# Row normalisation of a 1024 x 4096 array: loads spread over the SyncE and the ScalarE queue

## The chip, the cores and the metric

One core of one Trainium2 chip. The metric is the device time of one execution in microseconds (us), as a median over several executions. The profile is of one execution and covers some 1.7 us less than that time.

## The reference

Each row of `x` (1024 x 4096, float32) is divided by its Euclidean norm:

```python
norm = np.sqrt(np.sum(x ** 2, axis=axis, keepdims=True) + eps)   # axis = -1
return (x / norm).astype(np.float32)
```

16.78 MB are read and 16.78 MB written; there is no reuse.

## The kernel before

The 1024 rows make 4 tiles of 128 partitions x 2 rows (4 MB each, 32 KiB to a partition). All four tiles have a buffer of their own, so nothing waits for a buffer.

```python
    for i in range(n_tiles):                       # 4 loads, all issued at once
        xt = io.tile([P, R, D], mybir.dt.float32)
        nc.sync.dma_start(out=xt.rearrange("p r d -> p (r d)"), in_=x[i])
        xts.append(xt)

    for i in range(n_tiles):
        xt = xts[i]
        ssq = stats.tile([P, R], mybir.dt.float32)
        for r in range(R):                         # ScalarE: squares and their sum
            nc.scalar.activation(out=sq, in_=xt[:, r], func=...Square,
                                 accum_out=ssq[:, r : r + 1])
        ...                                        # ScalarE: square root; VectorE: reciprocal
        for r in range(R):                         # VectorE: scale in place
            nc.vector.tensor_scalar_mul(
                out=xt[:, r], in0=xt[:, r], scalar1=rstd[:, r : r + 1]
            )
        nc.sync.dma_start(out=out_t[i], in_=xt.rearrange("p r d -> p (r d)"))
```

## Time and profile before

| | before |
|---|---|
| time, median | 84.22 us (84.21 to 84.26, 3 runs) |
| span of the profile | 82.5 us |
| DMA engines busy | 96% of the span |
| ScalarE / VectorE busy | 41% / 23% |
| moved | 33.55 MB, 1024 packets of 32 KiB and 128 tiny ones |

In a row of tenths, each digit is the busy share of a fortieth of the span (2.06 us here); 9 is 90% or more. A line of the timeline begins with the start and the length of a piece of work; in brackets stands how long its engine was idle before it, and what ended that. DVE is VectorE, ACT is ScalarE; SPq and ACTq are the instruction queues of SyncE and ScalarE, where a `DMA_DIRECT2D` line is the handing over (the issue) of a transfer. `xt<-in_x_dram` is a load, `out_dram<-xt` a store. A transfer is moved in packets, here of 32 KiB, by the 16 DMA engines, and it has landed when its last packet is reported done. The slack of a store is how much later it could be issued without a DMA engine having to wait for it. The lines themselves are in the prediction.

### The profile page before, as it was taken

The numbers are of one execution on the slowest core, as the hardware profiler recorded it, in microseconds if no ns is written. First come the engines' busy times: TensorE is split into PE (matmuls) and PEld (weight loads), VectorE is DVE, ScalarE is ACT, GpSimd is POOL, SyncE is SP. The second block draws the span as 40 slices with busy tenths as digits, with TensorE's granted clock in tenths as the row PEclk, the third lists the DMA queues.
The fourth block names the chain that finished last, engine by engine and source line by source line (L and its number), as shares of the span: only waits on it lengthen the run. The fifth ranks groups of instructions, "written<-read, shape, count | busy, mean of one in ns | idle before, by whom it ended". The sixth has DMA issues, their size and how long they took to land.

```text
span 82.5 us, 98 instructions
## 1 busy us (share of the span) xinstructions
DVE 19.2 (23%) x13; ACT 33.4 (41%) x22; POOL 0.2 (0%) x4
## 2 busy tenths in 40 slices
DVE  0000000000299019910498003990000000000000
ACT  6000006999799982999519996000000000000000
POOL 0000000000000000000000000000000000000000
DMA  6689998996999899899979989998998998899890
GB/s 175 286 365 445 508 397 365 508 461 302 508 493 397 381 508 413 350 508 461 302 302 461 493 381 397 508 413 350 508 445 381 445 508 381 381 508 413 365 493 0
DMA packets 1152, 33.55 MB, mean 407 GB/s; under 512 B 128, under 2 KB 128, under 8 KB 128
## 3 DMA queue, kind: packets, MB, share of 16 engines
q1 hardware_dynamic: 1152, 33.55, 96.0%
HBM read 16.78 MB, written 16.78 MB: 407 GB/s over the span
## 4 chain that ended last, share of the span: by engine, by line
DMA 50%; ACT 9%; DVE 3%; DVEq 3%; SPq 1%; issue 0%
DMA xt<-in_x_dram 50%; ACT sq L53 9%; DVE xt L70 3%; DVEq L104 3%; SPq L46 1%; ACT rstd L61 0%; DVE rstd L67 0%
## 5 line engine op out<-in xcount | busy, mean ns | idle before, releaser
L53 ACT ACTIVATE sq<-xt 128x4096 f32<-128x4096 f32 x8 | 28.9, 3617 | 16.5 <-DMA xt<-in_x_dram 16.4
L70 DVE TENSOR_SCALAR xt<-xt,rstd 128x4096 f32<-128x4096 f32 x8 | 18.5, 2350 | 0.1
L67 DVE RECIPROCAL rstd<-rstd 128x2 f32<-128x2 f32 x4 | 0.7, 166 | 35.5 <-ACT rstd L61 35.5
L53 ACT ACT_TABLE_LOAD x1 | 1.3, 1283 | 0.7 <-PEq L90 0.7
L53 ACT ACTIVATION_READ_ACCUMULATOR sq<-xt 128x1 f32 x8 | 1.5, 186 | 0.0
L61 ACT ACT_TABLE_LOAD x1 | 1.3, 1283 | 0.0
L61 ACT ACTIVATE rstd<-ssq,eps_t 128x2 f32<-128x2 f32 x4 | 1.2, 296 | 0.1
L41 DVE MEMSET eps_t<- 128x1 f32 x1 | 0.1, 59 | 0.8 <-PEq L90 0.8
L90 POOL MEMSET const-bfloat16-1.0<- 128x1 bf16 x1 | 0.1, 102 | 0.0
L90 POOL MEMSET const-uint8-127<- 128x1 uint8 x1 | 0.1, 102 | 0.0
L90 POOL MEMSET const-float32-0.0<- 128x1 f32 x1 | 0.1, 99 | 0.2 <-issue 0.2
L90 POOL MEMSET const-float32-1.0<- 128x1 f32 x1 | 0.1, 99 | 0.0
## 6 DMA issues: line engine op xcount, KB each, us to landing
xt<-in_x_dram SPq DMA_DIRECT2D x4, 4096.0 KB, 26.2
out_dram<-xt SPq DMA_DIRECT2D x4, 4096.0 KB, 26.4
```

The costliest lines, as they stand in the source:

```text
L41: nc.vector.memset(eps_t, eps)
L46: nc.sync.dma_start(out=xt.rearrange("p r d -> p (r d)"), in_=x[i])
L53: nc.scalar.activation(out=sq, in_=xt[:, r], func=mybir.ActivationFunctionType.Square, accum_out=ssq[:, r : r + 1],)
L61: nc.scalar.activation(out=rstd, in_=ssq, func=mybir.ActivationFunctionType.Sqrt, bias=eps_t,)
L67: nc.vector.reciprocal(out=rstd, in_=rstd)
L70: nc.vector.tensor_scalar_mul(out=xt[:, r], in0=xt[:, r], scalar1=rstd[:, r : r + 1])
L90: nc = _bacc.Bacc("TRN2", target_bir_lowering=False, num_devices=1)
L104: with _tile.TileContext(nc) as tc:
```

## The change

Two queues hand loads to the DMA engines instead of one: tiles 0 and 2 by SyncE, tiles 1 and 3 by ScalarE. The intent is to have two loads in progress at once. Stores stay on SyncE.

```diff
+    queues = (nc.sync, nc.scalar)
     xts = []
     for i in range(n_tiles):
-        xt = io.tile([P, R, D], mybir.dt.float32)
-        nc.sync.dma_start(out=xt.rearrange("p r d -> p (r d)"), in_=x[i])
+        xt = io.tile([P, R, D], F32)
+        queues[i % 2].dma_start(
+            out=xt.rearrange("p r d -> p (r d)"), in_=x_t[i]
+        )
         xts.append(xt)
```

Cut: renames, and the pool of statistics that goes from 4 buffers to `n_tiles`, which is also 4.

More of the change, by code (lines that the diff above doesn't have):

```diff
@@ L20 @@
     P = nc.NUM_PARTITIONS
+    F32 = mybir.dt.float32
     assert isinstance(axis, int) and axis in (-1, len(x.shape) - 1)
@@ L31 @@
     n_tiles = N // (P * R)
-    x = x.rearrange("(t p r) d -> t p (r d)", p=P, r=R)
+    x_t = x.rearrange("(t p r) d -> t p (r d)", p=P, r=R)
     out_t = out_flat.rearrange("(t p r) d -> t p (r d)", p=P, r=R)
@@ L36 @@
     scratch = ctx.enter_context(tc.tile_pool(name="scratch", bufs=1))
-    stats = ctx.enter_context(tc.tile_pool(name="stats", bufs=4))
-    sq = scratch.tile([P, D], mybir.dt.float32)
-    eps_t = scratch.tile([P, 1], mybir.dt.float32)
+    stats = ctx.enter_context(tc.tile_pool(name="stats", bufs=n_tiles))
+    sq = scratch.tile([P, D], F32)
+    eps_t = scratch.tile([P, 1], F32)
     nc.vector.memset(eps_t, eps)
+    queues = (nc.sync, nc.scalar)
     xts = []
     for i in range(n_tiles):
-        xt = io.tile([P, R, D], mybir.dt.float32)
-        nc.sync.dma_start(out=xt.rearrange("p r d -> p (r d)"), in_=x[i])
+        xt = io.tile([P, R, D], F32)
+        queues[i % 2].dma_start(
+            out=xt.rearrange("p r d -> p (r d)"), in_=x_t[i]
+        )
         xts.append(xt)
@@ L50 @@
         xt = xts[i]
-        ssq = stats.tile([P, R], mybir.dt.float32)
+        ssq = stats.tile([P, R], F32)
         for r in range(R):
@@ L58 @@
             )
-        rstd = stats.tile([P, R], mybir.dt.float32)
+        rstd = stats.tile([P, R], F32)
         nc.scalar.activation(
```

## The prediction

> **What bounds the kernel now.** I read first what limits the whole span, then whether any stage has another limit, then how much spare time the compute has. The page of the kernel before comes first: busy shares, the DMA row of the 40 slices, packets and queues.
>
> ```profile
> span 82.5 us, 98 instructions
> DVE 19.2 (23%) x13; ACT 33.4 (41%) x22; POOL 0.2 (0%) x4
> ...
> DMA  6689998996999899899979989998998998899890
> ...
> DMA packets 1152, 33.55 MB, mean 407 GB/s; under 512 B 128, under 2 KB 128, under 8 KB 128
> q1 hardware_dynamic: 1152, 33.55, 96.0%
> ```
>
> No compute engine reaches half the span, and the 16 DMA engines are busy for 96% of it, with no gap in the row of tenths except at the two ends. 128 of the packets are tiny (the completion marks); the other 1024 carry 33.55 MB, so 32 KiB each, 64 on each engine. A mean packet takes 0.96 x 82.5 x 16 / 1024 = 1.237 us; the single packet records of the steady stretches stand at 1.213 us. 64 x 1.213 = 77.6 us of the 82.5 us span is therefore time in which each DMA engine moves bytes at its steady rate, and 16 x 32 KiB / 1.213 us is 432 GB/s. The rest of the span (4.9 us) is: 1.7 us until the first packet starts, some 0.8 us because first packets take about 2 us, 0.7 us where loads give way to stores (the loads land 9.7 us apart, the last one 10.4 us after its forerunner), some 0.35 us from the last packet to its landing, and 0.8 us of closing down. Another 84.2 - 82.5 = 1.7 us of the measured time lies outside the profiled span.
>
> Next the DMA issues and the waits, for where transfers sit in the queue.
>
> ```profile
> xt<-in_x_dram SPq DMA_DIRECT2D x4, 4096.0 KB, 26.2
> out_dram<-xt SPq DMA_DIRECT2D x4, 4096.0 KB, 26.4
> ```
>
> All eight transfers go through the one SyncE queue. A transfer of 4 MB needs about 9.7 us alone, yet a store needs 26.4 us from issue to landing, because it stands behind two others. The stores are issued early and queue: the compute is far ahead of the DMA. The timeline gives the slack.
>
> ```profile
> 0.73 1.28 ACT L53 ACT_TABLE_LOAD   x1 [0.73 <-PEq L90]
> 0.73 1.91 SPq L46 DMA_DIRECT2D xt<-in_x_dram  x4
> ...
> 13.07 3.62 ACT L53 ACTIVATE sq<-xt 128x4096 f32<-128x4096 f32 x1 [11.05 <-DMA xt<-in_x_dram]
> ...
> 20.54 1.28 ACT L61 ACT_TABLE_LOAD   x1
> ...
> 22.78 3.62 ACT L53 ACTIVATE sq<-xt 128x4096 f32<-128x4096 f32 x1 [0.65 <-DMA xt<-in_x_dram]
> ...
> 30.79 4.62 DVE L70 TENSOR_SCALAR xt<-xt,rstd 128x4096 f32<-128x4096 f32 x2
> ...
> 42.99 3.62 ACT L53 ACTIVATE sq<-xt 128x4096 f32<-128x4096 f32 x1 [2.71 <-DMA xt<-in_x_dram]
> ...
> 51.00 4.62 DVE L70 TENSOR_SCALAR xt<-xt,rstd 128x4096 f32<-128x4096 f32 x2
> ```
>
> The squares start at 13.07, 22.78, 32.51 and 42.99, each time when a load has landed. The stores issue at 27.00, 35.44, 45.16 and 55.65, and land at 52.7, 62.3, 72.0 and 81.7. The store queue's data starts only when the loads are done, near 42.5, and store k's turn comes near 42.5, 52.2, 61.9 and 71.6. A store needs about 1.0 us from issue to first packet (first load: issue 0.73, packet 1.74). So the slack of the four is about 14.5, 15.7, 15.7 and 14.9 us. The chain of waits puts only half of the span on the loads and stops at the last store's issue; the row of DMA tenths is what shows that the stretch from 56 to 82 us is DMA alone.
>
> **What the Trainium skill says.** The page "DMA: Bandwidth & Descriptors", section "Issuing engines are not separate DMA queues", says that transfers started by ScalarE, SyncE or GpSimd all end on the same 16 DMA engines and interleave, and that several issuers save only the sequencer's issue time. The trace of before cannot test that, as it has one queue, but shows what there is to save: an issue takes 0.38 to 0.53 us while a transfer lasts 9.7 us. The section "Where 436 GB/s comes from" of the same page sets the ceiling on the SBUF side at 435.2 GB/s; this trace's 432 GB/s in the steady stretches is 99.3% of it, so it agrees and leaves nothing to gain in rate. Its section "Queues, rings and completion order" (arbitration) says that each DMA engine takes packets from the queues that have work in turn; no run here shows that yet, and the prediction of landing times rests on it. Last, the table of "Latency and other measured facts" reports slow copies where partition rows lie 4 MiB apart in HBM (103 GB/s against 207); this is a rival below.
>
> **The change part by part.**
> Renames, the type alias and the moved comment cost nothing. The stats pool goes from 4 buffers to one per tile; 1024 rows / (128 x 2) is 4 tiles, so it stays 4. Instruction counts stay: 8 transfers of 4 MB, 8 squares, 4 square roots, 4 reciprocals, 8 scalings.
>
> Issue: SyncE loses two load issues (about 0.9 us) and ScalarE gains two. They are ahead of ScalarE's first square, with the 1.28 us table load: some 2.2 us of its first 22 us. Nothing waits for either. The first load still leaves SyncE at 0.73, so the first packet still starts near 1.7. Cost on the path: 0.
>
> Landing order: tiles 0 and 1 now share each DMA engine packet by packet, then tiles 2 and 3. Two tiles are 16 packets per engine, 19.4 us. So tile 0, which landed at 13.0, lands at about 21.5 to 22.8, together with tile 1 (22.8 before); tiles 2 and 3 land together at about 42 to 43 (32.5 and 43.0 before). ScalarE's first wait grows from 11 to about 20 us.
>
> Compute: from the first square to the store's issue is 27.00 - 13.07 = 13.93 us for the first tile (it has the table load of the square root), and 35.44 - 22.78 = 12.66 us for a later one. ScalarE is held by the first tile for 9.06 us (13.07 to 22.13), by a later one for 7.78 us (22.78 to 30.56). VectorE's part (0.17 + 4.62) is shorter and never holds it up.
> - tile 0: 22.6 + 13.93, store issued at 36.5
> - tile 1: ScalarE free at 31.7, + 12.66 = 44.3
> - tile 2: landed near 42.7, + 12.66 = 55.4
> - tile 3: ScalarE free at 50.5, + 12.66 = 63.2
>
> The stores come 9.5, 8.9, 10.2 and 7.5 us later than before. Now against the DMA: the loads still need 32 packets per engine and end near 42.5; the stores' turns stay at 42.5, 52.2, 61.9 and 71.6. With 1.0 us from issue to packet, the slack left is 5.0, 6.9, 5.5 and 7.4 us. All positive: the DMA engines never run dry, and the last store still lands near 81.7.
>
> Sum: issue 0, rate 0, compute delay 0 (about 5 us of it still hidden): 84.2 + 0 = 84.2 us.
>
> **The rivals.**
> 1. The compute delay becomes a hole in the DMA stream. For it: tile 0 lands nearly 10 us later, and the work now comes in two bursts of two tiles. Against it: the slack above. To lose 2% (1.7 us) a store would have to be 5.0 + 1.7 = 6.7 us later than worked out, almost a whole tile of ScalarE work. If the table load, the interleaving and the landing all went badly by 1 us, still nothing would show. If it held: 85 to 88 us.
> 2. Two streams slow the memory. For it: tiles 0 and 1 lie exactly 4 MiB apart, the distance at which the skill's table shows slow copies; and ends of loads already cost 0.7 us where reads and writes meet. Against it: that table is about 128 rows at once, here an engine alternates between two contiguous runs of 32 KiB, and the distance between partitions inside a tile is unchanged. A loss of 5% on the 39 us of loads would give 86.2 us; I give this 2 or 3 chances in 100.
> 3. Two queues hide something that one does not: the slow first packets (0.8 us) or the turn from loads to stores (0.7 us), or both queues feed the engines sooner at the start. All of it together is 1.5 us, less than 2%. Half of one of them would give 83.8 us. The packets of steady stretches follow one another without a gap, so there is nothing else for a second queue to fill.
> 4. The queues are not served in equal turns, so that tile 0 lands earlier, anywhere between 13 and 22.6. Then the slack is greater, and the time is 84.2 all the same.
>
> **Range and chances.** The centre is 84.2 us. Upward, the start of two rings and the mixed end of the loads could cost some tenths; downward rival 3 could give some tenths. Before varies by 0.05 us only. I set 83.6 to 84.8 for 8 in 10. Faster by over 2% would mean under 82.5 us: it needs all of rival 3 and more, 1 in 100. Slower by over 2% means over 85.9 us, rivals 1 and 2 together: 3 in 100. Within 2%: 96 in 100.
>
> **What would show it.** In the changed kernel's profile there should be two queues, of about 8.4 MB (ScalarE) and 25.2 MB (SyncE); the DMA row without a gap and near 96%; the first square near 22.6 instead of 13.07, with a wait of about 20 us; the last scaling near 58 to 63 instead of 51 to 55.6; stores that land some 16 to 19 us after issue instead of 26, since they wait less in the queue; and a span of 82.5 us. A first square at 13 would refute the equal turns, not the time. A hole in the DMA row between 42 and 72 us would mean that rival 1 holds, a row that is full but at less than about 410 GB/s before 42 us that rival 2 does. A span under 81.5 us would refute the claim that the DMA engines' rate leaves nothing to gain.

## The result

| | before | after |
|---|---|---|
| median | 84.25 us (6 runs) | 84.29 us (6 runs) |
| range | 84.21 to 84.36 | 84.23 to 84.58 |
| ratio | | 1.0006 (95%: 0.9994 to 1.0018) |

The time is the same. A ratio here is the mean time of one kernel's fast runs over that of the other's in the same rounds, so not quite the ratio of the medians.

The page of the changed kernel, with busy shares, the DMA row, the queues and the issues (the last figure of an issue is the median time from issue to landing):

```profile
span 82.5 us, 98 instructions
DVE 19.2 (23%) x13; ACT 33.2 (40%) x22; POOL 0.2 (0%) x4
...
DMA  6898996998999899699969989989999998999890
...
q1 hardware_dynamic: 864, 25.17, 71.7%
q10 hardware_dynamic: 288, 8.39, 24.4%
...
out_dram<-xt SPq DMA_DIRECT2D x4, 4096.0 KB, 17.3
xt<-in_x_dram ACTq DMA_DIRECT2D x2, 4096.0 KB, 32.0
xt<-in_x_dram SPq DMA_DIRECT2D x2, 4096.0 KB, 31.8
```

There are two queues now, and their shares add up to 96.1%, which the one queue had (96.0%). The span is the same. But stores need 17.3 us from issue to landing where they needed 26.4, and loads 32 where they needed 26. The single packets of steady stretches still take 1.213 us. The timeline shows what moved:

```profile
0.73 0.89 ACTq L47 DMA_DIRECT2D xt<-in_x_dram  x2
0.73 0.86 SPq L47 DMA_DIRECT2D xt<-in_x_dram  x2
...
1.65 1.28 ACT L56 ACT_TABLE_LOAD   x1 [1.65 <-PEq L93]
22.65 3.62 ACT L56 ACTIVATE sq<-xt 128x4096 f32<-128x4096 f32 x1 [19.72 <-DMA xt<-in_x_dram]
...
36.58 26.99 SPq L76 DMA_DIRECT2D out_dram<-xt  x4
...
42.92 3.62 ACT L56 ACTIVATE sq<-xt 128x4096 f32<-128x4096 f32 x1 [3.54 <-DMA xt<-in_x_dram]
...
58.60 4.62 DVE L73 TENSOR_SCALAR xt<-xt,rstd 128x4096 f32<-128x4096 f32 x2
```

The first square starts at 22.65 us, not at 13.07: tiles 0 and 1 land together (22.62 and 22.80), tiles 2 and 3 as well (42.90 and 43.07). The whole compute runs 8 to 10 us later, and the end does not move: store landings are 52.7, 62.4, 72.0 and 81.7 us against 52.7, 62.3, 72.0 and 81.7.

So two things need proof. First, that the DMA engines' work is the whole bound. Second, that the compute's delay was hidden by a slack of about 5 us that remains of some 14.5, and is not simply harmless.

### The profile page after: what moved, and what is told of

It is laid out like the page before. It is cut to its first block, busy times and chain, and to the rows that moved or that the text cites. A ratio compares the mean times of both kernels' runs of the same rounds, so it can differ in the third digit from the quotient of the medians.

```text
span 82.5 us, 98 instructions
## 1 busy us (share of the span) xinstructions
DVE 19.2 (23%) x13; ACT 33.2 (40%) x22; POOL 0.2 (0%) x4
## 2 busy tenths in 40 slices
DMA packets 1152, 33.55 MB, mean 407 GB/s; under 512 B 128, under 2 KB 128, under 8 KB 128
## 4 chain that ended last, share of the span: by engine, by line
DMA 51%; ACT 19%; DVE 3%; DVEq 3%; SPq 0%; issue 0%
DMA xt<-in_x_dram 51%; ACT sq L56 18%; DVE xt L73 3%; DVEq L107 3%; ACT rstd L64 1%; SPq L47 0%; DVE rstd L70 0%
## 6 DMA issues: line engine op xcount, KB each, us to landing
out_dram<-xt SPq DMA_DIRECT2D x4, 4096.0 KB, 17.3
```

## The experiments

The theory: the time is what the 16 DMA engines need for 33.55 MB; the change spends most of the slack between a store's issue and its turn. Rivals: some compute still lies on the path; two queues as such delay or slow something; the slack is untouched.

### No arithmetic at all

```diff
     for i in range(n_tiles):
         xt = xts[i]
-        ...  # squares, square root, reciprocal, scaling
         nc.sync.dma_start(out=out_t[i], in_=xt.rearrange("p r d -> p (r d)"))
```

> The kernel before without any arithmetic: each tile is stored as it was loaded (wrong result on purpose). If the bytes through the 16 DMA engines set the time, the span stays 82.5 us and the time 84.2 us (within 0.5%). A rival in which some of the compute still lies on the path would give less: up to 5 us less if a store's start waited for its tile.

Measured: 84.37 us (ratio 1.0008, 0.9997 to 1.002), with a wrong result, as meant. The page:

```profile
span 82.4 us, 54 instructions
...
DVE 0.1 (0%) x1; POOL 0.2 (0%) x4
...
DMA  7679998998998999799979998997998998899890
```

ScalarE has gone from the list and the DMA row looks as before. In the kernel before, the arithmetic costs nothing. That the same holds for the changed kernel, with its later stores, this run does not show.

### Two queues with the tile order kept

```diff
-        nc.sync.dma_start(out=xt.rearrange("p r d -> p (r d)"), in_=x[i])
+        nc.sync.dma_start(out=xt[:, 0], in_=x[i][:, :D])
+        nc.scalar.dma_start(out=xt[:, 1], in_=x[i][:, D:])
```

> The kernel before, each tile's load cut in two halves of 2 MB, one on SyncE and one on ScalarE: two queues, but the tiles' order kept. Theory (the landing order, not the number of queues, moves the compute): first square near 13, stores issued near 27, 35.4, 45.2 and 55.7 as in the kernel before, time 84.2. A rival in which two queues as such delay the tiles: first square well after 14.

Measured: 84.36 us (ratio 1.001, 0.9998 to 1.0022). From its timeline and page:

```profile
13.03 3.62 ACT L54 ACTIVATE sq<-xt 128x4096 f32<-128x4096 f32 x1 [8.94 <-DMA xt<-in_x_dram]
...
out_dram<-xt SPq DMA_DIRECT2D x4, 4096.0 KB, 26.4
```

With two queues the first square starts at 13.03 us, as with one, and a store waits 26.4 us again. The edit also halves the load packets to 16 KiB, and neither time nor landings show it. So it is not the second queue that delays the compute, but which tiles share the engines.

### How much slack is left: one, two and three spare squares

A spare square takes 3.74 us of ScalarE ahead of the first tile and leaves the result right. In front of the first tile's squares:

```diff
+        if i == 0:
+            spare = scratch.tile([P, 3], mybir.dt.float32)   # or 1, 2, 4
+            for k in range(3):
+                nc.scalar.activation(out=sq, in_=xt[:, 0], func=...Square,
+                                     accum_out=spare[:, k : k + 1])
```

The kernel before with three:

> The kernel before with three spare squares of 3.74 us (11.2 us together) in front of the first tile's squares. Its slack was worked out as 14.5 us, so theory: the store of tile 0 issued near 38.2, time 84.2. If the slack were smaller than 11.2 us, each us of the lack would show in the time.

The changed kernel with one, two and three:

> The changed kernel with one spare square (3.74 us) in front of the first tile's squares. Slack worked out: its store issues at 36.58, + 1.0 us to the first packet, against a turn near 42.4, so 4.8 us. Theory: 84.3, unchanged. The rival that the change leaves no slack gives about 88.

> The changed kernel with two spare squares (7.5 us). Theory: 2.7 us over the slack of 4.8 us, so a hole in the DMA row near 43 to 45 us and a time of 86.5 to 87.6 us. Rival (compute lies anywhere beside the DMA, the change did not touch the slack): 84.3.

> The changed kernel with three spare squares (11.2 us), the same that the kernel before gets in another run. Theory: 6.4 us over the slack, a hole of about that size and 90.2 to 91.3 us; the rival 84.3.

The form that keeps the tile order over two queues, with three:

> The form with each tile cut over both queues, with three spare squares (11.2 us). Theory (it keeps the tile order, so it keeps the slack of some 14.5 us): 84.2 to 84.4. Rival (two queues as such eat the slack): about 90, as the changed kernel with the same three squares.

| kernel | first store issued | time | ratio to before (95%) |
|---|---|---|---|
| before | 27.00 us | 84.25 us | |
| before, 3 spare | 38.14 | 84.07 | 0.9974 (0.9961 to 0.9987) |
| halves on both queues, 3 spare | 38.12 | 84.25 | 0.9974 (0.9934 to 1.0014) |
| changed | 36.58 | 84.29 | 1.0006 (0.9994 to 1.0018) |
| changed, 1 spare | 40.10 | 83.59 | 0.9906 (0.9859 to 0.9952) |
| changed, 2 spare | 43.81 | 86.79 | 1.0278 (1.0238 to 1.0319) |
| changed, 3 spare | 47.56 | 90.57 | 1.0725 (1.0683 to 1.0767) |

The DMA rows with three spare squares, first of the kernel before:

```profile
DMA  7689989997998998999998997997999899899890
```

of the halves on both queues:

```profile
DMA  4799999999999999999998997997999899799790
```

and of the changed kernel, where a slice is 2.22 us long:

```profile
DMA  7599988999988999983005969999789999599990
```

The same added work costs the first two kernels nothing. In the third the row falls to 3, 0, 0, 5 in slices 19 to 22 (40 to 49 us): the loads are done and no store is ready. That is the hole which the changed kernel was close to. The store of tile 0 was issued 7.23 and 10.98 us later than without spare squares, and the time rose by 86.79 - 84.29 = 2.50 and 90.57 - 84.29 = 6.28 us. The differences, 4.73 and 4.70 us, are the slack that the change had left, reckoned from its own time of 84.29 us; 4.8 was expected. Two of the three rivals fall here: the slack was touched, and not by two queues as such.

One row did not fit. With one spare square the changed kernel became faster, 83.59 us, where "unchanged" was expected. Reckoned from these 83.59 us, the time begins to rise earlier, at a delay of 7.23 - (86.79 - 83.59) = 4.0 us. How the agreement with the expected 4.8 us came about is said further down.

### Why a later store was faster

The packet records of these runs show where loads give way to stores. In the kernel before, the last two load packets of each engine took up to 2.14 us instead of 1.213; added up, that is 0.87 us for an engine (a mean over the 16). In the changed kernel it is 1.04 us. With one or two spare squares no load packet there is slow; with one, the first store packet of five engines is (up to 1.82 us, 0.15 us in the mean). A view of the stretch from 40 to 42 us shows the difference, though not the single packets; the last two figures are the busy share of the DMA engines and GB/s, first of the changed kernel, then with one spare square:

```profile
40.00:42.00 2.00, 2.00 (x2) 0.00 (x0) 0.00 (x0) 1.00 1.00 279
...
40.00:42.00 2.00, 0.07 (x1) 2.00 (x1) 0.00 (x0) 1.00 1.00 393
```

The engines count as fully busy in both: the busy share does not tell a slow packet from a quick one. The landings show the slow packets too. The times from issue to landing of the loads, in the kernel before:

```profile
DMA to landing us min/median/max: 12.3/26.2/40.9
```

in the changed kernel:

```profile
DMA to landing us min/median/max: 21.9/31.9/41.9
```

and in the changed kernel with one spare square:

```profile
DMA to landing us min/median/max: 21.7/31.3/40.8
```

The last load lands 1.1 us sooner after its issue when the first store is issued later. The new theory: the last one or two load packets ahead of an engine's first store packet are slow when that store is already waiting; a store that arrives just as the loads run out avoids it. It is not the issue of the store as such: in the kernel before it is issued at 27.00 us, and the first slow packet starts at 38.84. With three spare squares in that kernel (issued at 38.14) only the last load packet of each engine is slow. Nor is it the arithmetic: the kernel without any has slow packets of 0.85 us too.

If this holds, the kernel before, with its one queue, must be able to win the 0.7 us as well. Three and a half spare squares bring its first store to the same moment, four bring it a little too late:

```diff
+            spare = scratch.tile([P, 4], mybir.dt.float32)
+            for k in range(4):                  # the last one on half the columns
+                nc.scalar.activation(
+                    out=sq[:, : D if k < 3 else D // 2],
+                    in_=xt[:, 0, : D if k < 3 else D // 2], ...)
```

> The kernel before (one queue) with three and a half spare squares in front of the first tile, so that its store is issued near 40.2 us, as in the changed kernel with one spare square. If the 0.7 us that that run won comes from when the first store reaches the DMA queue, and not from two queues: 83.5 to 83.7 us. If two queues are needed for it: 84.1.

> The kernel before with four spare squares (15.0 us): first store issued near 41.9, first packet near 42.9, against loads that stop moving near 41.4 us. Theory: a short hole of about 1.5 us, without the slow turn (0.9 us): 84.5 to 85.0.

Measured with three and a half: first store issued at 40.08, 83.61 us (ratio 0.9901, 0.987 to 0.9932). No slow load packets near the turn are left, and the loads need:

```profile
DMA to landing us min/median/max: 12.1/26.1/39.9
```

39.9 us for the last load against 40.9 in the kernel before. Two queues are not needed for this. Of this 1.0 us, 0.7 reaches the end: the 32 store packets of an engine take 0.23 us longer in all than in the kernel before, and some engines wait up to 0.45 us for their first. With four squares: first store issued at 41.93, 84.83 us (ratio 1.0054, 1.0016 to 1.0092). Here the last load packets end between 41.1 and 41.7, the first store packets start at 42.8, and the hole costs more than the smooth turn saves. This also measures the slack of the kernel before: its store came 14.93 us later for a loss of 0.5 us (the ratio of 1.0054), so the slack, reckoned from its own time like the 4.7 us, is about 14.5 us, as worked out. So an issue near 40 us is close to the best moment, and an issue at 38.14 gains only a part (84.07 us; 0.58 us of slow packets).

### Can the gain be had without spare work?

Two kernels were to hold back the first store by a dependency: the last 8 columns of tile 0 are scaled in program order behind the reciprocal of a later tile, and its store follows.

```diff
+        if i == 2:      # in the changed kernel: 1
+            nc.vector.tensor_scalar_mul(
+                out=xt0[:, 1, D - 8 :], in0=xt0[:, 1, D - 8 :], scalar1=rstd0[:, 1:2])
+            for k in range(2):
+                nc.sync.dma_start(out=out_t[k], in_=...)   # the stores held back
```

Cut: the scaling of tile 0 leaves these 8 columns out, and the stores that are not held back are issued as before. In the changed kernel only the store of tile 0 is held back.

The kernel before, in this form:

> The kernel before without any added work: the scaling of the last 8 columns of tile 0 is put behind the reciprocal of tile 2, so that the stores of tiles 0 and 1 are issued one after the other near 40.6 us instead of 27.0 and 35.4. If the slow load packets come from stores that queue up behind the last loads: 83.4 to 83.7 us, faster than both kernels by 0.7 to 0.9%. If not: 84.2.

The changed kernel, in this form:

> The changed kernel with the same trick: the last 8 columns of tile 0 are scaled behind the reciprocal of tile 1, so its store is issued near 39.8 instead of 36.6 us. If the moment of the first store sets the turn's cost: 83.6 to 83.9; if not: 84.3.

Measured: 84.31 us (ratio 0.9982, 0.9955 to 1.0008) and 84.34 us (0.9984, 0.9958 to 1.001). That is no verdict on the theory, because the edit did not hold anything back. The timeline of the second one:

```profile
36.24 0.22 DVE L75 TENSOR_SCALAR xt<-xt,rstd 128x8 f32<-128x8 f32 x1
36.49 0.35 SPq L79 DMA_DIRECT2D out_dram<-xt  x1
...
39.18 0.17 DVE L70 RECIPROCAL rstd<-rstd 128x2 f32<-128x2 f32 x1 [2.72 <-ACT rstd L64]
```

The 8 columns were scaled at 36.24 us, before the reciprocal at 39.18 that they stood behind in the program: nothing but program order linked the two, and in the built kernel they ran in the other order. The store went out at 36.49, as ever; in the first kernel at 27.20. A true data dependency would be needed. This one attempt at a version without spare work failed, and whether one can win the 0.7 us is not shown; the two fastest kernels measured, 83.59 and 83.61 us, are correct but compute squares that nobody uses.

### Loads and stores on different queues

```diff
-        nc.sync.dma_start(out=xt.rearrange("p r d -> p (r d)"), in_=x[i])
+        nc.scalar.dma_start(out=xt.rearrange("p r d -> p (r d)"), in_=x[i])
```

All four loads go to ScalarE, the stores stay on SyncE.

> The kernel before with all four loads on the ScalarE queue and the stores on SyncE, so that stores need not stand behind loads. If the queues take equal turns and the rate is the bound: store 0 lands near 48 us instead of 52.7, the last load near 55 instead of 43, the store of tile 3 is issued near 68 with 1 to 2 us to spare, and the time stays 84.2. If mixing reads and writes hides the turn from loads to stores (about 0.7 us): 83.5. If mixing costs rate: over 85. If the last store comes late: 85 to 87.

Measured: 84.50 us (ratio 1.0023, 1.0008 to 1.0038). Its issues:

```profile
xt<-in_x_dram ACTq DMA_DIRECT2D x4, 4096.0 KB, 28.0
out_dram<-xt SPq DMA_DIRECT2D x4, 4096.0 KB, 24.1
```

The last load landed at 55.32 and the last store was issued at 67.99, both as expected. Store 0 landed at 51.66, not at 48: it was issued at 27.11, but all but two of its first packets, one to an engine, started after 32.4 (the first of all at 31.12). From there 8 packets in equal turns take 16 x 1.213 = 19.4 us, which gives its landing. The slow load packets came in this run too, with starts between 29.0 and 32.7 us (0.98 us per engine), just ahead of each engine's first packet of store 0. After that, loads and stores ran side by side for 20 us at 1.213 us a packet. So in this run the mixture of reads and writes is not slow in itself; it is their first meeting that costs about 1 us, once.

## Why the prediction was right

- **The bound.** The DMA engines at 432 GB/s set the time: shown by the kernel without arithmetic (84.37 us) and by the end that stays when the compute moves. But 84.2 us is not the least time for these bytes: 83.6 was measured. The five parts that the prediction gives for the 4.9 us beside the steady packets add up to 4.35 us only. The trace has the rest: the engines start at 2.05 us in the mean, not all at 1.74, and end at 81.03 in the mean, the last at 81.33.
- **Issue costs nothing.** ScalarE's table load moved from 0.73 to 1.65 us and nothing waited for it; ScalarE's first wait still ended with a landing. Argued before, and seen in the timeline.
- **Equal turns.** 21.5 to 22.8 us was predicted for tiles 0 and 1, and 22.62 and 22.80 measured. Rival 4 (unequal turns) is out.
- **Store issues.** 36.5, 44.3, 55.4 and 63.2 predicted; 36.58, 44.26, 55.58 and 63.24 measured. From issue to landing 16 to 19 us predicted; 16.1 to 18.4 measured.
- **Slack.** 5.0 us for the first store predicted; 4.7 measured by the spare squares. Rival 1 had the right mechanism and nearly the right threshold: a loss of 1.7 us was to need a delay of 6.7 us; by the measured slack it needs 6.4 (7.23 us gave 2.50). That the figures agree so well hides an error: the store's turn at 42.5 us has the slow load packets in it, and with a late store the loads stop at 40.9 to 41.4 us instead. So the DMA engines begin to wait after some 4.0 us, and it takes 4.7 until that has used up what the quick packets save.
- **Rival 2**, slow memory for two streams 4 MiB apart: the packets still take 1.213 us. Not seen.
- **Rival 3** named the slow first packets and the slow turn from loads to stores as all there was to gain, but it tied that gain to the second queue. The changed kernel does not have the gain (1.04 us of slow packets, 0.87 before), and one queue can have it. The prediction also counted the turn as a fixed part of the span; it hangs on when the first store arrives. That this did not touch the predicted time was luck: the changed kernel's store comes at 36.58 us and still meets the slow turn; at 40.1 us the time was 83.59, just below the stated range of 83.6 to 84.8.

What stays open: why load packets take longer when a store waits behind them. The runs show when it happens and what it costs, not what in the DMA engine does it.

## What to carry to other kernels

Here one queue kept the DMA engines full, and a second one added no bandwidth (ratio 1.0006); it changed which transfers share the engines, and so when each one landed. If tiles are to be worked on in order, let them land in order: keep one queue, or cut each tile over both rather than alternate tiles, or the slack of the compute shrinks (here from some 14.5 to 4.7 us) without any sign in the time. To see that a change was harmless rather than merely hidden, add known work and look for the point where the time begins to rise.

## What the Trainium skill lacked or had wrong

- "DMA: Bandwidth & Descriptors", "Issuing engines are not separate DMA queues": right that a second issuer brings no bandwidth (ratio 1.0006), but it does not say that landing order changes: tile 0 landed at 22.62 us instead of 13.04, and 11.2 us of added work cost 6.3 us instead of nothing.
- Same page, "Queues, rings and completion order": equal turns agree with the landings. It lacks how long a queue that joins late waits for its first turn: issued at 27.11 us, 14 of the 16 first packets started after 32.4 us.
- No page that I read has the cost of the first stores meeting running loads: 0.85 to 1.04 us per DMA engine, once, and at most 0.15 us when the first store is issued at about 40 us, where the loads run out.
- Same page, "Where 436 GB/s comes from": its sentence that for transfers between HBM and SBUF the HBM side of about 358 GB/s binds is not true of this run, with one core at work: 407 GB/s over the span and 432 in steady stretches, near the 435.2 of the SBUF side. The page's own measured table has 425 GB/s for a core whose neighbour is idle, so only this sentence lacks the condition that both cores of the pair are at work.
- Same page, "Latency and other measured facts": its slow copies at a pitch of 4 MiB are of 128 partition rows at that pitch, so no error; it lacks what two streams 4 MiB apart do. They were not slow here (1.213 us a packet, with one stream or two).
